# Layer B's keys and values by seven products for eight, for all heads, ahead of the attention

## The chip, the cores and the metric

The kernel runs on one core of one Trainium2 chip. The metric is the device time of one execution in microseconds (us). Before the change the median of three runs is 2861.07 us (2860.74 to 2862.50). The profile shown is of one execution of its own, which took 2862.76 us; the span from its first to its last instruction is 2861.1 us.

## The reference, cut to what matters

One step of a small encoder with two layers over 640 tokens (512 of a new stream, 16 each of 8 running streams), model width 2048. Layer A is a pooling mixer with an input projection 2048 -> 8192, four group maps and an output projection 4096 -> 2048. Then keys, values and one forget logit per head are made of the stream, and layer B attends to them:

```python
hk = rmsnorm(x, norm_kv)
kvf = hk @ w_kv                              # 2048 -> 16 heads x 128 keys, the same of values, 16 logits
k = kvf[..., :W_B].reshape(B, T, N_HEADS, HEAD_DIM)
v = kvf[..., W_B:2 * W_B].reshape(B, T, N_HEADS, HEAD_DIM)
logf = jax.nn.log_sigmoid(kvf[..., 2 * W_B:] + b_f)
...
F_all = jnp.cumsum(logf_all, axis=1)
for l in range(N_B):                         # one layer
    h = rmsnorm(x, norm_b[l])
    z = h @ w_in_b[l]                        # query and gate, 2048 each
    o = fox_attention(q, k_all, v_all, Fq, F_all, q_pos, k_pos)
    x = x + (o * jax.nn.silu(gate)) @ w_out_b[l]
return rmsnorm(x, norm_f), k, v, logf, ...
```

Keys, values and log forget values are outputs too. A running stream also attends to 256 cached rows per head. All matrices are float32.

## The kernel before

All activations lie with features on the 128 partitions and the 640 tokens along the row, as two halves of 320. Every large product is made of three TensorE products, from a value split into a rounded part "h" and a rest "l": h with h, h with l, l with h. `split` (L80) makes the two parts: ScalarE writes the rounded copy (L81), VectorE subtracts it (L84). One TensorE matmul here is a 128x128 block of a weight by 320 tokens.

**Layer A.** `pair8` (L244) makes 256 columns of an output by a scheme with seven block products in place of eight (Strassen-Winograd): the input's 2048 rows are four slabs, and in each slab the loop goes over seven products and two row blocks, three matmuls each: 42 matmuls a slab, 168 for a pair of column blocks. The seven results lie in PSUM banks 0 to 6 until `combine` (L263) adds them up on VectorE, after one ScalarE copy (L275). The weights of a slab arrive as one DMA of 512 KB into `raw` (three buffers, `fetch` L181), and `prep` (L196) makes their sums (VectorE L201, L203, L204) and splits all seven blocks (L81, L84). `advance` (L219) keeps this up to three or four slabs ahead, and `wbufs` (L188) hands out the buffers in turn, three in the input projection (loads 0 to 127, `NA`), four after it. The activations' seven blocks (`Side` L143) are split ahead: three in the tiles "bh", "bl", four sums in "th", "tl".

In the input projection `u_pair` (L493) and `gate_pair` (L595) alternate, 32 pairs in four groups of the pooling; a u pair ends in running sums on GpSimd (L545), one more of them in each later group. Group maps use `plain` (L626), without the seven products: 96 matmuls for 256 columns. The output projection uses the seven products for the first three groups (`out_pair` L662) and `plain` for the last (`last_pair` L763), eight pairs of 14 us each. `last_pair` adds its product to the stream that it has read back from memory, stores it, takes squares for the norm (ScalarE, then a sum on GpSimd, L740) and splits it into the operands of layer B (`split_x` L744; for the second half of the blocks after the loop).

**Layer B before the change.** `proj` (L864) makes 128 columns of a projection of the whole stream: 16 row blocks by three products by two halves, 96 matmuls (`mm3` L814, L817). `chunk` (L859) brings a quarter of the weights at a time (DMA of 256 KB, L832), scales it by the norm's gain (VectorE L838) and splits it (L846, L848), two chunks ahead. Each head has four such projections, of keys (`k_block` L939), values (`v_block` L949), gate (`gate_block` L1111) and query (`q_block` L1097). The norm's factor R of each token is multiplied onto the result. Keys and values are turned with VectorE's 32x32 transposes and stored as output rows (`key_rows`, `v_rows`); values come back from memory with tokens on partitions.

Attention of a head (`attn` L1142) is a Python generator. It is cut into 17 pieces by `yield`, and `tick` (L88) runs the next piece; `proj` calls `tick` after every second row block, that is every 12 matmuls, or calls `next` on the rows' generator. So a head's attention (scores of the cache L1150 and of new tokens L1158 to L1162, softmax, transposes L105, values L1249 to L1263) is woven into the key and value projections of the next head.

`forget` (L971) makes the forget logits once, at the start of layer B: 32 narrow matmuls by the float32 stream (L1018, `acc` is the whole stream, read back), logarithms and running sums.

**Order.** TensorE's program is in the order written (`manual_schedule`). For the other engines and the DMA queue of SyncE (SP) a planner puts instructions in order by its own costs; each engine then runs its list in order. Memory of a pool that was closed is handed on tile by tile when the last reader of each tile is done.

After layer B the output projection (L1321, 512 columns a matmul) and the last norm follow.

Of the kernel before, what the change touches and what calls it, by code (L numbers as in the profile page):

```python
# [39 lines left out]
def tile_yoco_step(ctx, tc, i, o):  # L40
# [89 lines left out]
    xt_ = pool(ctx, "xt")  # L130
    sa = ctx.enter_context(ExitStack())
    wa, xb_, misc = pool(sa, "wa"), pool(sa, "xb"), pool(sa, "misc")

    def tslot(j, part, shape, dt=F32):
        return xt_.tile(shape, dt, tag=f"t{part}{j}", name=f"t{part}")

    def bslot(j, part, shape, dt=F32):
        return xb_.tile(shape, dt, tag=f"b{part}{j}", name=f"b{part}")
# [16 lines left out]
    def blocks_b(sd, x4):  # L155
        sd.bh, sd.bl = (bslot(sd.j, q, [P, 3, HALF], F32R) for q in "hl")
        nc.scalar.activation(sd.bh, x4[:, 1:4, :], AF.Copy)
        nc.vector.tensor_tensor(sd.bl, x4[:, 1:4, :], sd.bh.bitcast(F32), op=ALU.subtract)
# [18 lines left out]
    NA = 128  # L177
# [9 lines left out]

    def wbufs(n, shape):  # L188

        j = n % 3 if n < NA else (2, 0, 3, 1)[(n - NA) % 4]  # L190
# [3 lines left out]
        return None, [[bslot(k, q, [shape[0], 1] + shape[2:], F32R) for k in range(2)] for q in "hl"]  # L194
# [24 lines left out]
    def advance():  # L219

        d = ndone[0]
        ahead = 3 if d < NA else 4
        while nprep[0] < min(d + ahead, len(loads)):
            if nload[0] <= nprep[0]:
                fetch()
            prep()
# [17 lines left out]
    def pair8(hook=None):  # L244

        pp = {m: banks[:, j, :] for j, m in enumerate(ORDER)}
        for s in range(4):
            wts = parts.pop(0)
            advance()
            for j, m in enumerate(ORDER):  # L250
                for kk in range(2):
                    product(pp[m], m, wts, kk, xs_[2 * s + kk], s + kk == 0, s == 3 and kk == 1)
                if j == 6:
                    done()
                if hook is not None:
                    hook(s, j)
# [43 lines left out]


# [5 lines left out]
    rows.append([bslot(4 + q // 2, "hl"[q % 2], [P, 512]) for q in range(4)])  # L307
    x4s = [tslot(4 + j // 2, "hl"[j % 2], [P, 4, HALF]) for j in range(7)] + [x4slot()]
    gains = [bslot(j, q, [1, 512]) for j in (2, 3) for q in "hl"]
    ones, idle = bslot(6, "h", [1, P]), bslot(6, "l", [P, P])  # L310
    ssq, tiny = bslot(7, "h", [P, TT, 4]), bslot(7, "l", [P, TT, 3])
# [314 lines left out]
    def plain(xk):  # L626
# [4 lines left out]
        for b in range(2):  # L631
            bk = [bank()[:, :HALF], bank()[:, :HALF]]
# [29 lines left out]
    def out_pair(g, c):  # L662
# [41 lines left out]
        o3 = bslot(2, "hl"[c % 2], [P, 3, HALF])  # L704
# [19 lines left out]
    ps_ = pool(sa, "ps_")  # L724
# [7 lines left out]
    xh, xl = [None] * KT, [None] * KT  # L732
    sqd = dram.tile([P, NT], F32, name="sqd")
    sqs = []

    def squares(k, x):
        s = bslot(2, "hl"[k % 2], [P, NT]) if k else misc.tile([P, NT], F32, tag="cve", name="sq")
        nc.scalar.activation(s, x, AF.Square)
        if k:
            nc.gpsimd.tensor_tensor(sqs[0], sqs[0], s, op=ALU.add)  # L740
        else:
            sqs.append(s)

    def split_x(k, x):  # L744

        t = tslot(k // 2, "hl"[k % 2], [P, 2, NT], F32R)
        xh[k], xl[k] = t[:, 0, :], t[:, 1, :]
        split(xh[k], xl[k], x)

    late = []  # L750

    def load_stream_pair(c):
        if c == 3:
            x1 = [bslot(3, q, [P, NT]) for q in "hl"]
        else:
            x1 = m4slot() if c in (2, 6) else x4slot() if c == 7 else ps_.tile([P, 4, HALF], F32, tag="sg", name="x1", bufs=2)
            x1 = x1.rearrange("p (k s) n -> p k (s n)", k=2)
            x1 = [x1[:, 0, :], x1[:, 1, :]]
        for k in range(2):
            dma(x1[k], xacc[c][k * P : (k + 1) * P, :])  # L760
        return x1

    def last_pair(c, x1, yk):  # L763
        pp = plain(yk)
        for b in range(2):
            a = halves(x1[b])
            for s in range(2):
                nc.vector.tensor_tensor(a[:, s, :], a[:, s, :], pp[b][s], op=ALU.add)
            k = 2 * c + b
            dma(xacc[c][b * P : (b + 1) * P, :], x1[b])  # L770
            squares(k, x1[b])
            if k < 8:
# [656 lines left out]
```

## Time and profile before

| stretch | us from the start | what runs |
|---|---|---|
| layer A, input projection | 0 to about 890 | 31 pairs by seven products, the first pair plain |
| layer A, group maps and output | 890 to 1524 | `plain`, `out_pair`, from about 1412 `last_pair` |
| layer B, keys, values, gate, query, attention | 1528 to 2633 | 64 projections and 16 heads |
| output projection and last norm | 2633 to 2861 | L1321 |

| | before |
|---|---|
| median of the runs | 2861.07 us |
| the profiled execution | 2862.76 us |
| its span | 2861.1 us |
| TensorE busy | 2800.3 us (98%) |
| VectorE, ScalarE, GpSimd busy | 65%, 35%, 11% |
| granted clock of TensorE, mean | 0.992 |

In the profile PE is TensorE, PEld its loading of weights, DVE VectorE, ACT ScalarE, POOL GpSimd and SP SyncE. A row of a group names the line, the engine, the operation, what is written and read, and how often. The end of a matmul is modelled, and matmuls overlap, so their pace is read from one start to the next and not from their durations. The row of a stretch gives for each engine its busy time and number of instructions, then TensorE's granted clock (1.00 is full), the busy share of the DMA engines and GB/s.

### The profile page before, as it was taken

Reading aid. Unit: us, or ns where it says so; the run is one execution under the profiler, and the core shown is the slowest. Engines: PE = TensorE matmul, PEld = TensorE weight load, DVE = VectorE, ACT = ScalarE, POOL = GpSimd, SP = SyncE. Lnnn points to the kernel's source line nnn. Section 1 sums busy time; section 2 is a strip of 40 time slices with the busy share of each in tenths; the row PEclk is TensorE's granted clock in tenths of the full one; section 3 lists DMA queues with packets and bytes.
Section 4 is the critical chain, followed back from the end, with each engine's and each line's share of the span. In section 5 each row is a group of like instructions: output and inputs, shape, how many; then the busy total and the mean of one; then the engine's idle time right before and its main releaser. Section 6 shows DMA issues by size and latency. Waiting matters only on the chain. (4 is left out here: it accounts for less than half of the span.)

```text
span 2861.1 us, 46583 instructions
## 1 busy us (share of the span) xinstructions
PE 2800.3 (98%) x18578; PEld 2698.3 (94%) x18578; DVE 1872.7 (65%) x3253; ACT 996.3 (35%) x1633; POOL 323.6 (11%) x333
## 2 busy tenths in 40 slices
PE   7899999999999999999999999999999999999998
PEld 6799999999999999999998999999999999999887
DVE  7877778888776848495445665566666665556434
ACT  5433333333333534343232233333333333334222
POOL 2212122232340110202021000000000000000000
PEclk9899999999999999999999999999999999999999
DMA  3344444444335786868636555444554545455833
GB/s 126 108 138 126 133 127 121 139 123 128 115 107 186 184 169 177 174 178 177 178 128 179 134 127 124 119 116 114 124 121 115 124 119 120 118 122 112 143 88 108
DMA packets 677058, 384.08 MB, mean 134 GB/s; under 512 B 323364, under 2 KB 634068, under 8 KB 676712
## 3 DMA queue, kind: packets, MB, share of 16 engines
q1 hardware_dynamic: 657256, 327.36, 43.2%
q0 software_dynamic: 19584, 53.75, 8.6%
q8 instruction: 145, 2.38, 0.3%
q14 instruction: 73, 0.60, 0.1%
HBM read 298.30 MB, written 82.71 MB: 133 GB/s over the span
## 5 line engine op out<-in xcount | busy, mean ns | idle before, releaser
L237 PE MATMUL banks<-th,wh 128*128 128x320 f32 x1280 | 404.9, 316 | 4.6 <-DVE cu L279 2.8
L817 PE MATMUL banks<-th,whi 128*128 128x320 f32 x2048 | 399.8, 317 | 3.5 <-ACT whi L846 3.5
L237 PE MATMUL banks<-th,wl 128*128 128x320 f32 x1280 | 400.2, 313 | 2.8 <-DVE wl L84 2.8
L237 PE MATMUL banks<-tl,wh 128*128 128x320 f32 x1280 | 399.8, 312 | 0.5 <-DVE tl L84 0.5
L817 PE MATMUL banks<-tl,whi 128*128 128x320 f32 x2048 | 385.0, 310 | 0.0
L848 DVE TENSOR_TENSOR wlo<-raw,whi 128x512 fp32r<-128x512 f32 x272 | 186.8, 687 | 216.0 <-ACT whi L846 212.8
L817 PEld LDWEIGHTS banks<-th,whi 128*128 128x128 f32 x2048 | 316.3, 189 | 9.7 <-ACT whi L846 3.8
L817 PEld LDWEIGHTS banks<-tl,whi 128*128 128x128 f32 x2048 | 322.9, 189 | 0.0
L237 PE MATMUL banks<-bh,wh 128*128 128x320 f32 x960 | 298.3, 311 | 14.6 <-ACT cve L275 10.7
L846 ACT ACTIVATE whi<-raw 128x512 fp32r<-128x512 f32 x272 | 171.6, 632 | 381.8 <-PE banks L817 226.7
L237 PE MATMUL banks<-bl,wh 128*128 128x320 f32 x960 | 297.6, 310 | 0.0
L237 PE MATMUL banks<-bh,wl 128*128 128x320 f32 x960 | 297.5, 310 | 0.0
L81 ACT ACTIVATE wh<-raw 128x768 fp32r<-128x768 f32 (+1 forms) x200 | 177.0, 887 | 336.8 <-issue 159.9
L84 DVE TENSOR_TENSOR wl<-raw,wh 128x768 fp32r<-128x768 f32 (+1 forms) x200 | 209.9, 1051 | 115.9 <-ACT wh L81 115.4
L81 ACT ACTIVATE wh<-sums 128x1024 fp32r<-128x1024 f32 x160 | 168.6, 1054 | 244.3 <-DVE sums L204 244.2
L237 PEld LDWEIGHTS banks<-th,wh 128*128 128x128 f32 x1280 | 244.4, 191 | 8.1 <-DVE cu L279 4.0
L237 PEld LDWEIGHTS banks<-th,wl 128*128 128x128 f32 x1280 | 244.2, 191 | 3.3 <-DVE wl L84 3.3
L237 PEld LDWEIGHTS banks<-tl,wh 128*128 128x128 f32 x1280 | 244.6, 191 | 0.8 <-DVE tl L84 0.8
L817 PE MATMUL banks<-th,wlo 128*128 128x320 f32 x1024 | 234.2, 310 | 2.0 <-DVE wlo L848 2.0
L84 DVE TENSOR_TENSOR wl<-sums,wh 128x1024 fp32r<-128x1024 f32 x160 | 202.9, 1268 | 48.0 <-ACT wh L81 47.6
L817 PE MATMUL banks<-tl,wlo 128*128 128x320 f32 x1024 | 234.1, 310 | 0.0
L237 PEld LDWEIGHTS banks<-bh,wh 128*128 128x128 f32 x960 | 181.3, 189 | 16.2 <-ACT cve L275 11.8
(407 smaller groups left out, 5285.9 us busy)
## 6 DMA issues: line engine op xcount, KB each, us to landing
raw<-in_w_in_a SPq DMA_DIRECT2D x128, 512.0 KB, 4.0
raw<-in_w_out_a SPq DMA_DIRECT2D x64, 512.0 KB, 4.7
raw<-in_w_kv SPq DMA_DIRECT2D x128, 256.0 KB, 3.2
raw<-in_w_in_b SPq DMA_DIRECT2D x128, 256.0 KB, 3.0
raw<-in_w_grp_a SPq DMA_DIRECT2D x32, 512.0 KB, 5.8
kc<-in_cache_k SPq DMA_DIRECT2D x64, 256.0 KB, 4.3
vc<-in_cache_v SPq DMA_DIRECT2D x16, 1024.0 KB, 7.6
raw<-in_w_out_b SPq DMA_DIRECT2D x64, 256.0 KB, 3.0
```

The source lines that it names most:

```text
L81: a = nc.scalar.activation(hi, x, AF.Copy)
L84: nc.vector.tensor_tensor(lo, x, hi.bitcast(F32), op=ALU.subtract)
L237: nc.tensor.matmul(bank[:, :HALF], w[kk][:, a, :], x, start=first and q == 0, stop=last and q == 2)
L817: nc.tensor.matmul(acc_[:, s, :HALF], w, x[:, s * HALF : (s + 1) * HALF], start=f, stop=l)
L846: nc.scalar.activation(hi, raw, AF.Copy)
L848: nc.vector.tensor_tensor(lo, raw, hi.bitcast(F32), op=ALU.subtract)
```

## The change

- **Keys and values first.** After layer A's last product a new stretch makes keys and values of all heads with `pair8` and `combine`: 16 calls of `kv_pair`, each two heads' keys or two heads' values. Their weights become 64 more loads of the list that layer A uses, of kind "s" (sums); `prep` scales them by the norm's gain with four ScalarE instructions ahead of the sums. `place` now says which weight buffer a load uses and which load has to be done before it.
- **The stream's operands** are the seven blocks of `Side` (`blocks_b`, `sums_t`, `split_t`), made during and after the eight `last_pair`s; `split_x` goes. Sums of sides 6 and 7 run on GpSimd. `last_pair` reads and stores the stream in one DMA each instead of two.
- **Result of a pair:** R is multiplied on by one GpSimd instruction on 128x1280; `rows_out`, one more generator, turns the result, stores keys to the outputs and to a scratch in memory (`kscr`), and values to a scratch (`sv`).
- **The forget logits'** narrow matmuls move into the `last_pair`s (`forget_sums`: four matmuls in each of the next one, on two instead of four column groups in turn); the rest of `forget` and the norm's factor run as pieces during the first pairs.
- **The attention part** has only the query and the gate as projections, 32 in place of 64. Each `proj` runs nine pieces (the last gate 16), after row blocks 0, 2, 4, 6, 8, 9, 11, 13 and 15. A head's attention starts in its own gate's projection and ends in the next head's query. The DMAs and splits that fetch the next head's keys, values, sums and cache stand at fixed places in `attn`.
- **Memory:** the operands are kept as "bh"/"bl" tiles (`xb_`) plus one more block per side (`last_blocks`, read back from memory during the last pair); `stream` picks the block. `R` and the running sums go through memory to the next part. The output projection's operands take over these places.

```diff
+    kvs = [(q, m) for m in range(8) for q in range(2)]
+    LAST = (3, 0, 1, 2)
+    for q, m in kvs:
+        for s in LAST if (q, m) == kvs[-1] else range(4):
+            c0 = q * D + m * 2 * P
+            loads.append(("s", wkv[:, 4 * s : 4 * s + 4, c0 : c0 + 2 * P], nkv_c[:, 4 * s : 4 * s + 4]))
...
     def prep():
         n = nprep[0]
-        raw = loaded.pop(n).rearrange("p (a b) (s n) -> p a (b s) n", a=2, n=P)
+        raw = loaded.pop(n)
+        if len(loads[n]) > 2:
+            for k in range(4):
+                nc.scalar.activation(raw[:, k, :], raw[:, k, :], AF.Copy, scale=loads[n][2][:, k : k + 1])
+        raw = raw.rearrange("p (a b) (s n) -> p a (b s) n", a=2, n=P)
...
+    def forget_sums(c):
+        for k in (2 * c, 2 * c + 1):
+            q = k % 4
+            for n in range(2):
+                nc.tensor.matmul(banks[32 * q : 32 * q + 32, 6 + n, :HALF], wr[0][:, k * H : k * H + 32],
+                                 stage[c][:, k % 2, n * HALF : (n + 1) * HALF], start=k < 4, stop=k >= 12)
...
-                last_pair(c, x1s[c], yk)
+                    load_stream_pair(q)
+                if c == 0:
+                    load_forget()
+                last_pair(c, yk)
+                if c:
+                    sums_t(x4of(c - 1)) if c < 7 else None
+                if 0 < c < 5:
+                    split_t(xs_[c - 1], x4of(c - 1))
         dk = nd
-    dma(sqd, sqs[0])
-    for k, x in late:
-        split_x(k, x)
+    for j in range(4, 7):
+        if j == 6:
+            blocks_b(xs_[j], x4of(j))
+            sums_t(x4of(j), None, nc.gpsimd)
+        split_t(xs_[j], x4of(j))
...
+    def kv_pair(n, q, m):
+        def hook(s, j):
+            if (n, s, j) == (0, 0, 2):
+                last_rows()
+            if (n, s, j) == (15, 2, 0):
+                last_blocks()
+
+        pp = pair8(hook, LAST if n == 15 else range(4))
...
+        t = x4slot()
+        combine(pp, lambda name: [(t[:, WHERE[name], :], slice(0, HALF))])
+        t = t.rearrange("p (k s) n -> p k (s n)", k=2)
+        nc.gpsimd.tensor_tensor(t, t, R.unsqueeze(1).to_broadcast([P, 2, NT]), op=ALU.mult)
+        work.insert(0, rows_out(q, m, t))
...
-    def proj(also=None):
+    def proj(ticks=9):
         pp = mmbank()
         for c in range(4):
             wh, wl = (w.rearrange("p (k n) -> p k n", n=P) for w in chunk())
             for k in range(4):
                 kk = 4 * c + k
-                mm3(pp, wh[:, k, :], wl[:, k, :], xh[kk], xl[kk], kk == 0, kk == KT - 1)
-                if kk % 2:
-                    if also is not None and kk > 1:
-                        next(also, None)
-                    if also is None or kk != 3:
-                        tick()
+                mm3(pp, wh[:, k, :], wl[:, k, :], kk, kk == 0, kk == KT - 1)
+                if kk * ticks % KT < ticks:
+                    tick()
         return pp
...
+        q_ = []
+        work.append(attn(0, q_))
         for h in range(H):
+            q_.extend(q_block(h))
             if h:
-                ks_ = k_block(h)
-                kc = load_keys(h)
-                vt = v_block(h, ks_[0])
-                sums = load_sums(h)
-                v, q_ = [], []
-                rows_ = v_rows(h, vt, v)
-                if h < H - 1:
-                    gate_block(h - 1, rows_)
-                vc = load_values(h)
-            work.append(attn(h, *ks_, v, q_, sums, kc, vc))
-            if h:
-                q_.extend(q_block(h))
-        gate_block(H - 2, rows_)
-        gate_block(H - 1)
+                work.append(attn(h, q_))
+            gate_block(h)
+            q_ = []
+        while work:
+            tick()
```

The step that follows `last_pair(7)` in the new order, run after the first 18 matmuls of the first key pair:

```diff
+    def last_rows():
+
+        forget_sums(7)
+        nc.scalar.activation(lt[:, :HALF], banks[:, 6, :HALF], AF.Copy)
+        nc.vector.tensor_copy(lt[:, HALF:], banks[:, 7, :HALF])
+        blocks_b(xs_[7], x4of(7))
+        sums_t(x4of(7), None, nc.gpsimd)
+        split_t(xs_[7], x4of(7))
```

More of the change, by code (lines that the diff above doesn't have):

```diff
@@ L631, in plain @@
         for b in range(2):
-            bk = [bank()[:, :HALF], bank()[:, :HALF]]
+            if c is None:
+                bk = [bank()[:, :HALF], bank()[:, :HALF]]
+            else:
+                bk = [banks[:, (4 * c + 2 * b + s) % 6, :HALF] for s in range(2)]
+            if b and c:
+                forget_sums(c - 1)
             for k in range(8):
```

564 lines of the change are left out of this document (301 added, 263 removed).

## The prediction

> **What bounds the kernel now.** I read the page's busy times first, then the chain of waits through layer B, then the stretches, and last the idle time before matmuls.
>
> ```profile
> PE 2800.3 (98%) x18578; PEld 2698.3 (94%) x18578; DVE 1872.7 (65%) x3253; ACT 996.3 (35%) x1633; POOL 323.6 (11%) x333
> ```
> ```profile
> 1832.12 29.91 PE banks L817 x204
> ```
> ```profile
> 1899.90 29.91 PE banks L817 x204
> ```
> ```profile
> 1000.00:1100.00 100.00, 100.00 (x684) 100.00 (x684) 60.81 (x98) 35.94 (x51) 15.17 (x15) 1.00 0.71 162
> 1764.35:1832.12 67.77, 67.77 (x476) 65.07 (x476) 40.45 (x80) 21.75 (x42) 0.00 (x0) 1.00 0.50 120
> 1794.26:1832.12 37.86, 37.86 (x272) 35.35 (x273) 25.25 (x55) 12.73 (x28) 0.00 (x0) 1.00 0.48 105
> ```
>
> TensorE ends every wait. A head takes 1899.90 - 1832.12 = 67.78 us, and TensorE is never idle in it. A projection's matmul costs 29.91/204 = 0.1466 us; in the stretch of layer A, where `out_pair` runs by seven products, 100/684 = 0.1462, so the two forms cost the same. A head's four projections are 384 x 0.1466 = 56.3 us, which leaves 11.5 us of attention matmuls. The last row is the part of a head in which its attention is woven in: as full as the rest, with VectorE busy for 25.25 of 37.86 us.
>
> **The change part by part.** The sum is made against the profiled span, 2861.1 us. That execution took 2862.76 us, 1.7 more than its span and 1.7 more than the median of the runs, so a span of 2861.1 stands for a median of 2861.07 and differences carry over.
>
> *Products.* Keys and values were 32 x 96 = 3072 matmuls; 16 pairs of 168 are 2688. 384 x 0.1466: **-56.3 us**. The weights' multiplication in gate and query stays.
>
> *The turn into layer B goes.*
>
> ```profile
> 1528.10 0.87 PE L817 MATMUL banks<-th,whi 128*128 128x320 f32 x4 [3.49 <-ACT whi L846]
> 1530.94 0.64 PE L817 MATMUL banks<-th,wlo 128*128 128x320 f32 x1 [1.96 <-DVE wlo L848]
> 1597.54 0.39 PE L1160 MATMUL banks<-kh,qh 128*128 128x256 f32 x1 [1.77 <-DVE pr L1164]
> ```
> ```profile
> 1530.00:1536.40 6.40, 5.46 (x20) 5.47 (x21) 4.46 (x9) 1.47 (x3) 5.14 (x17) 0.50 0.97 292
> 1560.00:1630.55 70.55, 68.78 (x510) 63.32 (x509) 43.82 (x104) 16.87 (x35) 0.00 (x0) 0.98 0.65 139
> ```
>
> TensorE idles 3.49 + 1.96 us and then runs 6.4 us at half clock, worth 3.2: 8.7. Head 0's first scores wait 1.77 more, and the clock of 0.98 over 70.55 us is another 1.4. I take **-11.9**.
>
> *Forget logits.*
>
> ```profile
> 1564.45 4.51 PE banks L1018 x64
> ```
> ```profile
> L1018 PE MATMUL banks<-acc,wr x64: 432/433/457, 1564.4 to 1568.5; 128*32 128x320 f32 x64
> ```
> ```profile
> 1861.97 1.06 PE L1150 MATMUL banks<-kct,qs 128*32 128x256 f32 x8
> 1862.96 0.49 PE L1158 MATMUL banks<-kt,qt 128*128 128x128 f32 x2
> ```
>
> The 64 instructions now come eight at a time, two column groups in turn instead of four. The cache scores L1150 have just that pattern: 8 in 0.99 us at 256 tokens, so 1.24 at 320, times 8 is 9.9 us. Bounds: the old pace, 4.5, and no overlap at all, 64 x 0.433 = 27.7. Net **+5.4** (0 to +23).
>
> *A steady key or value pair.* VectorE has per slab `prep`, per pair `combine` and two transposes; GpSimd has the product with R.
>
> ```profile
> L84 DVE TENSOR_TENSOR wl<-sums,wh 128x1024 fp32r<-128x1024 f32 x36 | 44.1, 1224 | 8.7 <-ACT wh L81 8.4
> L84 DVE TENSOR_TENSOR wl<-raw,wh 128x768 fp32r<-128x768 f32 x36 | 34.3, 954 | 22.7 <-ACT wh L81 22.7
> L201 DVE TENSOR_TENSOR sums<-raw 128x512 f32<-128x512 f32 x47 | 32.4, 689 | 9.4 <-DMA raw<-in_w_out_a 8.7
> L204 DVE TENSOR_TENSOR sums<-raw,sums 128x256 f32<-128x256 f32 x47 | 19.8, 422 | 0.7
> L203 DVE TENSOR_TENSOR sums<-sums,raw 128x256 f32<-128x256 f32 x47 | 19.8, 421 | 0.5
> ```
> ```profile
> L279 DVE TENSOR_TENSOR cu<-cu,banks 128x320 f32<-128x320 f32 x31 | 14.9, 482 | 0.0
> L934 DVE STREAM_TRANSPOSE kn<-kt 128x640 f32<-128x640 f32 x16 | 13.4, 836 | 0.0
> L740 POOL TENSOR_TENSOR sq<-sq,bl 128x640 f32<-128x640 f32 x8 | 14.0, 1754 | 90.4 <-ACT bl L738 90.4
> L545 POOL TENSOR_TENSOR sw<-sw 128x772 f32<-128x772 f32 (+2 forms) x48 | 85.6, 1783 | 4.8 <-DMA dscr<-dd 1.4
> L846 ACT ACTIVATE whi<-raw 128x512 fp32r<-128x512 f32 x272 | 171.6, 632 | 381.8 <-PE banks L817 226.7
> ```
>
> VectorE: 4 x 3.71 + 7 x 0.482 + 2 x 0.836 = 19.9 us beside 168 x 0.1466 = 24.6 us of TensorE. GpSimd: 128x1280, twice L740, 3.5 us. These two disturb each other:
>
> ```profile
> 685.80 6.17 POOL L545 TENSOR_TENSOR sw<-sw 128x772 f32<-128x772 f32 x3
> ```
> ```profile
> 686.84 1.84 DVE L201 TENSOR_TENSOR sums<-raw 128x512 f32<-128x512 f32 x1
> 688.72 1.57 DVE L203 TENSOR_TENSOR sums<-sums,raw 128x256 f32<-128x256 f32 x1
> 690.33 1.93 DVE L204 TENSOR_TENSOR sums<-raw,sums 128x256 f32<-128x256 f32 x1
> ```
>
> Beside GpSimd's sums the operations of 0.689, 0.421 and 0.422 us take 1.84, 1.57 and 1.93. So I count both engines' work in a row: 19.9 + 3.5 = 23.4 of 24.6 us, still under TensorE. The Trainium skill speaks against this part: "SBUF — State Buffer", section "Who interferes with whom", says that a VectorE instruction with two inputs in SBUF and a GpSimd one that reads SBUF block each other fully. By that rule too the sum in a row, 23.4, would hold, and the pair would stay TensorE's; the trace's tripled durations agree.
>
> ScalarE gets four 128x256 instructions a slab, each under the 0.632 of 128x512, at most 10 us a pair, spread over an engine that is busy for a third. The row stores move here too:
>
> ```profile
> L930 SPq DMA_DIRECT2D out_k_prompt<-kn x64: 327/490/1122, 1557.3 to 2563.5; - x64
> ```
>
> For a key pair SP issues 16 of these (8 for values), a store to the scratch and four weight loads, 21 x 0.49 = 10 us of its 24.6; a store queued ahead of a load waits for GpSimd and a transpose, some 6 us after the pair's end, and the weights are fetched up to three slabs, 18 us, ahead. I add 0.3 us a pair for waits on banks: **+4.5** (0 up to the first rival's price).
>
> *The new turn, `last_pair(7)` to the first key pair.* Nothing is spare here. Sides 4 to 7 are split late, since their places hold the last product's operands. From the end of that product until slab 3 of the first pair, 3 x 6.2 + 1.2 = 19.7 us later, VectorE and GpSimd have:
>
> ```profile
> L158 DVE TENSOR_TENSOR bl<-m,bh 128x960 fp32r<-128x960 f32 x12 | 13.9, 1156 | 0.0
> L84 DVE TENSOR_TENSOR tl<-draw,th 128x1280 fp32r<-128x1280 f32 x16 | 23.8, 1489 | 6.7 <-ACT th L81 6.7
> ```
>
> two `blocks_b` (2 x 1.156), two splits (2 x 1.489), two preps (2 x 3.71), two sums on GpSimd (8 halves of L740, 7.0), one square (1.75), two adds (1.0): 22.5 us, and the norm's factor beside it. Late by 3 to 6 us, then `forget`'s small operations in pairs 1 and 2 while VectorE has 1.2 us a pair to spare, and one or two stretches at half clock (1.5 each, below). I take **+10**, from 2 (hidden but for one bank wait) to 22 (all exposed). Queued behind each late VectorE subtraction are the next preps, and TensorE waits for them in order. What covers this work otherwise is TensorE's own 24.6 us of the first pair.
>
> *The turn into the attention part.* The new weight buffers lie where side 0's sums were, whose last reader is the second of four slabs of the last pair, 12 us before its end; so the first chunks can be split ahead. **+2.5** (0, to the old turn's 8.7).
>
> *Attention with half the projections.* 192 x 0.1466 + 11.5 = 39.6 us a head, already in the sum, if nothing waits. The quoted 37.86 us stretch is nearly this loop: two projections with the attention's pieces 12 matmuls apart, no idle time.
>
> ```profile
> L848 DVE TENSOR_TENSOR wlo<-raw,whi 128x512 fp32r<-128x512 f32 x272 | 186.8, 687 | 216.0 <-ACT whi L846 212.8
> L838 DVE TENSOR_TENSOR raw<-raw,cols 128x512 f32<-128x512 f32 x256 | 169.7, 678 | 5.3 <-DMA raw<-in_w_kv 3.9 <-DMA raw<-in_w_in_b 0.9
> ```
>
> VectorE drops by 8 x 1.365 and four operations of 0.84, from 40.4 to 26.1 us of 39.6, 66%, as in that stretch (67%). SP loses eight weight DMAs and 16 row stores a head; the value load's store behind its own load stays, and weights are two chunks, some 9 us, ahead of it. **+3** for 16 heads (0 to 32). The last head runs pieces 6 matmuls apart: **+2** (0 to 8).
>
> Sum: -56.3 - 11.9 + 5.4 + 4.5 + 10 + 2.5 + 3 + 2 = -40.8, so **2820 us**.
>
> **The rivals.**
>
> *Every pair stalls at its boundary (slower).* Layer A's fourth group does so:
>
> ```profile
> 415.16 0.42 ACT L275 ACTIVATE cve<-banks 128x320 f32<-128x320 f32 x1
> ```
> ```profile
> 465.00 0.42 ACT L275 ACTIVATE cve<-banks 128x320 f32<-128x320 f32 x1
> ```
> ```profile
> 697.86 0.42 ACT L275 ACTIVATE cve<-banks 128x320 f32<-128x320 f32 x1
> ```
> ```profile
> 752.98 0.42 ACT L275 ACTIVATE cve<-banks 128x320 f32<-128x320 f32 x1
> ```
> ```profile
> 698.34 0.41 PE L237 MATMUL banks<-bh,wh 128*128 128x320 f32 x1 [2.54 <-ACT cve L275]
> ```
> ```profile
> 699.70:703.10 3.40, 3.40 (x14) 3.40 (x15) 3.40 (x9) 0.53 (x1) 0.00 (x0) 0.56 0.35 120
> ```
>
> ScalarE's copy L275, behind a split that waits for VectorE, holds bank 0; TensorE idles 2.54 us and then loses 44% of 3.4 us, 1.5. Two units take 55.1 us (752.98 - 697.86) instead of 49.8 (465.00 - 415.16): 5.3 a stall. On all 16 pairs: 2820 - 4.5 + 85 = 2900. From 8 stalling pairs on, the gain is gone. For it: ScalarE has more ahead of its copy now. Against it: in a row, two units of that group have 36.4 us of VectorE and 14.3 of eight GpSimd sums, over TensorE's 49.3; two key pairs have 46.8. (On the clock, "TensorE: Matmul & The Clock Gate", section "HAM oscillation", of the Trainium skill asks for gaps above about 3.4 us; by it this stall would cost 2.5 only. The trace shows half clock after 2.54, and I price by the trace.)
>
> *Attention's own latency bounds a head.* With no plain projections between, a late softmax is never caught up. One wait like the 1.77 at head 0 in each head: +28 - 3, 2845. For it, that wait; against it, the 14 later heads without any.
>
> *The new turn is hidden.* Planner and buffers cover it: +2 for it, none at boundaries: 2807.
>
> **How the numbers follow.** Forecast with its own range 2808 to 2834: 0.68; hidden turn or better, 0.12; attention latency, 0.10; boundary stalls, 0.08, of which some stop short of slower; anything else 0.02. A measurement here can tell 0.2%, 6 us. Slower needs over 47 us against the sum: 0.06; the same 0.03; faster 0.91. The range 2800 to 2845 reaches over the hidden turn and attention latency and leaves boundary stalls out.
>
> **What would show it.** Right: 16 key and value pairs with starts 24.6 to 25.5 us apart after the first two; heads 39.6 to 40 us apart with TensorE full; about 10 us of idle and half clock in the first 50 us after the last L638 matmul; eight groups of forget matmuls of 1.2 us. Wrong: waits of TensorE for L275 in most pairs, a head above 41 us, or a granted clock below 0.98 in either part.

## The result, and the profile after

The changed kernel takes 2910.95 us (median of four runs, 2910.45 to 2913.13) against 2861.78 for the kernel before beside it: a ratio of 1.0171, 95% interval 1.0153 to 1.0189. It is slower by 1.7%; 2820 had been predicted. The profiled execution took 2911.26 us, its span 2909.3. Two executions of the experiments took far longer than the others of their kernel, 8918.69 us in run 9 and 3500.23 in run 12, and are left out of the medians given below.

The page's row of busy times, as it was shown of before:

```profile
PE 2780.2 (96%) x18194; PEld 2651.2 (91%) x18194; DVE 2014.5 (69%) x3430; ACT 1149.5 (40%) x1911; POOL 382.2 (13%) x357
```

The 384 matmuls are gone (18578 to 18194), but TensorE is busy for 96% instead of 98%: it waits. Four stretches, by engine (length; busy time and count of PE, PEld, DVE, ACT, POOL; clock; DMA):

```profile
1532.40:1630.00 97.60, 87.73 (x571) 84.65 (x571) 82.23 (x140) 51.74 (x87) 25.42 (x25) 0.95 0.40 99
1630.00:1955.00 325.00, 322.91 (x2163) 316.94 (x2163) 267.30 (x369) 172.41 (x304) 38.67 (x18) 1.00 0.52 122
1955.40:2073.80 118.40, 103.46 (x686) 95.07 (x685) 66.57 (x139) 36.06 (x72) 3.17 (x2) 0.96 0.61 146
2161.37:2248.98 87.61, 80.90 (x566) 73.78 (x565) 53.77 (x120) 33.04 (x66) 0.00 (x0) 1.00 0.54 130
```

The first is the turn from layer A into the first pairs of keys and values, the second is the rest of that part, nearly full. The third is the start of the attention part, the fourth two of its heads: 87.6 us at full clock, of which TensorE is idle for 6.7. VectorE is busy for 61% there, ScalarE for 38%, so no engine is at its limit.

To see where the 89 us between forecast (2820.3 of span) and result lie, I divide the span at TensorE's wait behind the last `last_pair` (1534.94 - 2.27 = 1532.67; before, 1528.10 - 3.49 = 1524.61) and at its wait for the attention part's first weights (1961.35 - 5.66 = 1955.69). TensorE's larger waits of the first turn and the first of the second (in brackets the idle time and what ended it):

```profile
1534.94 0.53 PE L251 MATMUL banks<-b,wh 128*128 128x320 f32 x2 [2.27 <-DVE x L802]
1544.66 1.41 PE L877 MATMUL banks<-sq,ones 128*128 128x320 f32 x2 [2.79 <-DVE lt L866]
1570.56 0.41 PE L251 MATMUL banks<-th,wh 128*128 128x320 f32 x1 [1.80 <-DVE cu L290]
1575.50 0.64 PE L251 MATMUL banks<-th,wh 128*128 128x320 f32 x1 [2.25 <-DVE cu L293]
1961.35 0.63 PE L1069 MATMUL banks<-th,whi 128*128 128x320 f32 x1 [5.66 <-ACT whi L1098]
```

The output projection of the kernel before starts at 2632.7 (its first row, below), 228.4 us ahead of the end, and I take as much off the end here. (That is a convention: a few of its matmuls now stand among the last head's work, from 2662.8 on.)

```profile
L1321 PEld LDWEIGHTS banks<-whi,th x240: 186/188/192, 2632.7 to 2794.9; 128*128 128x128 f32 x120
```

| stretch | forecast, us | measured, us |
|---|---|---|
| layer A to its end | 1534.5 (1524.6 + 9.9) | 1532.7 |
| keys and values | 408.6 (394.1 + 10 + 4.5) | 423.0 |
| attention part | 648.8 (the rest of the sum) | 725.2 (2909.3 - 228.4 - 1955.7) |

So 76 of the 89 us lie in the attention part. Its row holds the turn into it (+2.5 in the sum) and the last head (+2) too, but most of the 76 belongs to the term for all heads that I had put at +3. A steady head there (one row of VectorE's list, the gate's product, per head) takes 44.25 and 43.36 us and not 39.6:

```profile
2157.13 0.83 DVE L1371 TENSOR_TENSOR og<-og,sgb 128x640 f32<-128x640 f32 x1 [4.07 <-ACT og L1367]
2201.38 0.83 DVE L1371 TENSOR_TENSOR og<-og,sgb 128x640 f32<-128x640 f32 x1 [4.07 <-ACT og L1367]
2244.74 0.83 DVE L1371 TENSOR_TENSOR og<-og,sgb 128x640 f32<-128x640 f32 x1 [4.07 <-ACT og L1367]
```

TensorE's waits over the attention part up to 2640, grouped (total, times, longest):

```profile
PE banks L1069 <- ACT whi L1098: 36.0, 23, 5.7
PE banks L105 <- DVE pr L1259: 20.0, 14, 2.0
```

A projection's matmul (L1069) waits for ScalarE's rounded weights, and a transpose (L105) for a softmax row. With two single waits of 1.8 and 0.9 us these make 58.7 us; what else the 76 are made of was not taken apart, and half clock behind some waits is a part of it (0.96 granted in the third stretch). Now one wait for weights, followed back through the lists of PE, ScalarE, VectorE and SyncE:

```profile
2207.01 0.41 PE L1069 MATMUL banks<-tl,whi 128*128 128x320 f32 x1 [1.08 <-ACT whi L1098]
```
```profile
2206.33 0.63 ACT L1098 ACTIVATE whi<-raw 128x512 fp32r<-128x512 f32 x1 [2.60 <-DVE raw L1090]
```
```profile
2197.02 0.29 DVE L1353 COPY ob<-banks 128x128 f32<-128x128 f32 x1 [5.09 <-PE banks L1351]
...
2202.30 0.49 DVE L1187 SCALAR_TENSOR_TENSOR qt<-banks,R 128x320 f32<-128x320 f32 x1
...
2204.37 1.30 DVE L1232 STREAM_TRANSPOSE kct<-kc 128x512 f32<-128x512 f32 x2
2205.59 0.65 DVE L1090 TENSOR_TENSOR raw<-raw,cols 128x512 f32<-128x512 f32 x1
```
```profile
2182.41 1.28 SPq L1084 DMA_DIRECT2D raw<-in_w_in_b  x1
2188.55 2.50 SPq L1084 DMA_DIRECT2D raw<-in_w_in_b  x3
```
```profile
DMA to landing us min/median/max: 3.3/3.5/3.7
```

Four loads of chunks of weights are issued between 2182.41 and 2191 and land 3.3 to 3.7 us later (the last row is of these four). VectorE idles 5.09 us ahead of 2197.02 and, by the row of 2201.38 shown above, 4.07 us more, with the first chunk there since about 2186. But in its list the scale of the first chunk (L1090) stands behind the head's last products, the query's parts and two key transposes, at 2205.59, some 20 us after landing; ScalarE and TensorE wait behind it. The Trainium skill ("PSUM — Partial Sum Buffer", section "Engine vs sequencer instructions") calls the queues of ScalarE, VectorE and GpSimd strictly first in, first out; the trace agrees, as the ready scale does not pass the copy that waits 5.09 us.

### The profile page after: what moved, and what is told of

The parts are those of the page before. It is cut to its first block, busy times and chain, and to the rows that moved or that the text cites. A ratio compares the mean times of both kernels' runs of the same rounds, so it can differ in the third digit from the quotient of the medians.

```text
span 2909.3 us, 46312 instructions
## 1 busy us (share of the span) xinstructions
PE 2780.2 (96%) x18194; PEld 2651.2 (91%) x18194; DVE 2014.5 (69%) x3430; ACT 1149.5 (40%) x1911; POOL 382.2 (13%) x357
## 5 line engine op out<-in xcount | busy, mean ns | idle before, releaser
L251 PE MATMUL banks<-b,wh 128*128 128x320 f32 x2688 | 602.7, 311 | 16.7 <-ACT cve L289 10.6
L251 PE MATMUL banks<-th,wh 128*128 128x320 f32 x1792 | 566.9, 316 | 9.5 <-DVE cu L293 4.6
L251 PE MATMUL banks<-tl,wh 128*128 128x320 f32 x1792 | 557.6, 311 | 0.7 <-DVE tl L84 0.7
L251 PEld LDWEIGHTS banks<-b,wh 128*128 128x128 f32 x2688 | 452.5, 189 | 18.3 <-ACT cve L289 11.6
L251 PE MATMUL banks<-b,wl 128*128 128x320 f32 x1344 | 417.2, 310 | 0.0
L1069 PE MATMUL banks<-b,whi 128*128 128x320 f32 x1536 | 358.0, 317 | 0.0
L1069 PEld LDWEIGHTS banks<-b,whi 128*128 128x128 f32 x1536 | 257.8, 191 | 1.2 <-issue 0.4
L251 PEld LDWEIGHTS banks<-b,wl 128*128 128x128 f32 x1344 | 254.1, 189 | 0.0
L1069 PE MATMUL banks<-b,wlo 128*128 128x320 f32 x768 | 197.7, 312 | 0.0
L217 DVE TENSOR_TENSOR sums<-raw 128x512 f32<-128x512 f32 x236 | 174.9, 741 | 11.5 <-POOL sq L769 4.5
L1069 PEld LDWEIGHTS banks<-b,wlo 128*128 128x128 f32 x768 | 135.4, 190 | 0.0
```

What stands on the lines that cost most here:

```text
L217: nc.vector.tensor_tensor(sums[:, :, 0:2, :], raw[:, :, 1:3, :], raw[:, :, 0:1, :].to_broadcast([P, 2, 2, P]), op=ALU.subtract)
L251: nc.tensor.matmul(bank[:, :HALF], w[kk][:, a, :], x, start=first and q == 0, stop=last and q == 2)
L1069: nc.tensor.matmul(acc_[:, s, :HALF], w, stream(k, q, s), start=f, stop=l)
```

## The experiments

**Theories.** A: the order of VectorE's list is the loss; there is time enough. B: the softmax chains stand too densely, now that half the projections are gone, whatever the list. C: weights come late, because of the queue (C1) or too few buffers (C2).

**1. Program order for VectorE and ScalarE in the attention part.**

```diff
+        listed = ExitStack()
+        listed.enter_context(tc.manual_schedule(engines={mybir.EngineType.DVE, mybir.EngineType.Activation}))
         work.append(attn(0, q_))
```

> The changed kernel (2911 us) with one edit: in layer B's attention part VectorE and ScalarE run their instructions in the order in which the program issues them, and not in the planner's. Theory A (the weights' scale and split stand too late in VectorE's planned list, behind the query's parts and the key turns; VectorE has time enough): the three waits of a head for the rounded weights (1.08, 1.50 and 1.08 us) go, a head falls from 44.2 to 40 to 41 us, and the time to about 2850. Theory B (the softmax chains stand too densely for one wait after another, whatever the list): heads stay at 44 and the time at 2900 to 2920. If program order puts the softmax chains ahead of the weights' work instead, the time rises above 2920, and the list still decides.

3062.48 us, ratio 1.0701 (1.0683 to 1.0719). The last case of the expectation: the list decides, but this one is worse. Waits for rounded weights are gone but for the first (5.7 us), and TensorE waits for other things:

```profile
PE banks L105 <- DVE ptl L1270: 57.9, 23, 4.7
PE banks L1237 <- DVE kct L1232: 38.2, 12, 4.4
```

**2. Without the scale.**

```diff
-            nc.vector.tensor_tensor(r, r, braws[n][1].unsqueeze(2).to_broadcast([P, 4, P]), op=ALU.mult)
```

> The changed kernel with the multiplication of layer B's gate and query weights by the norm's gain left out (the output is another one): 8 multiplications of VectorE fewer per head. Theory A: the multiplication is the late link ahead of the rounding on ScalarE, so the waits for the rounded weights shrink or go and the time falls by 30 to 55 us, to 2856 to 2880. Theory B: VectorE is loaded to 61% in a head and the wait for a softmax row stays: the time falls by less than 15 us.

2909.51 us, 1.0169 (1.0148 to 1.0190): the time is the same, though VectorE has eight instructions of some 0.65 us less per head. The waits have moved:

```profile
PE banks L105 <- DVE pr L1258: 34.3, 14, 2.6
PE banks L1069 <- ACT whi L1097: 11.6, 16, 3.8
```

Those for rounded weights fell from 36.0 to 11.6 us, as A expected, and those for a softmax row rose from 20.0 to 34.3. The time is B's number. It removes the narrow form of A, that the scale by itself is the late link.

**3 and 4. More buffers.** Four instead of three for the rounded weights and rests, with three chunks prepared ahead instead of two; then seven instead of four for the incoming weights, with seven loads ahead (the main lines of each):

```diff
-        hi, lo = (wp.tile([P, 512], F32R, tag=q, name=q, bufs=3) for q in ("whi", "wlo"))
+        hi, lo = (wp.tile([P, 512], F32R, tag=q, name=q, bufs=4) for q in ("whi", "wlo"))
```
```diff
-            raw = wp.tile([P, 512], F32, tag="raw", name="raw", bufs=4)
+            raw = wp.tile([P, 512], F32, tag="raw", name="raw", bufs=7)
```

> The changed kernel with four buffers instead of three for the rounded and the rest weights, and three chunks prepared ahead of the first projection instead of two: a chunk is prepared one chunk of products (some 4.8 us) earlier. Theory A: a late scale then costs no wait; the time falls by 30 to 60 us, to 2850 to 2880. Theory B: no change beyond 10 us.

> The changed kernel with seven buffers instead of four for the weights as they come from memory, so that a chunk's load is issued three chunks (some 15 us) earlier. Theory C (the loads come late, behind other loads in SyncE's queue): the waits go and the time falls by 30 to 60 us. Theories A and B: the loads are there in time already, and the time moves by less than 10 us.

The first gives 2902.75 us, 1.0139 (1.0123 to 1.0154), 8 us less: again B's number. Its waits for rounded weights are nearly gone, but others stand in their place:

```profile
PE banks L105 <- DVE pr L1258: 20.0, 15, 1.6
PE banks L105 <- DVE ptl L1269: 15.5, 15, 1.0
PE banks L1069 <- ACT whi L1098: 7.2, 2, 5.7
```

These are softmax rows, rests of the turned softmax, and the weights. The second run gives 2868.09 us, 1.0017 (1.0008 to 1.0027), 43 us less than the changed kernel. That looked like C. But its list had changed as well: three scales in a row stand now at 2173.73, ahead of the head's end (L1371) by 15 us.

```profile
2173.73 1.88 DVE L1090 TENSOR_TENSOR raw<-raw,cols 128x512 f32<-128x512 f32 x3
...
2188.68 0.83 DVE L1371 TENSOR_TENSOR og<-og,sgb 128x640 f32<-128x640 f32 x1 [4.07 <-ACT og L1367]
```
```profile
PE banks L1237 <- DVE kct L1232: 19.6, 15, 4.5
```

What is left, but for the first wait of 5.7 us and two for a softmax row (2.8), are the waits for turned keys at a head's start.

**5, 6 and 8. Less to load; the scale issued earlier; the kernel before with more buffers.** Runs 5 and 6:

```diff
-                load_keys(h + 1)
+                cached[h + 1] = cached[h]
...
-            if more:
-                load_values(h + 1)
```
```diff
         split_next()
+        for n in range(3):
+            scale_next(n)
         fetchb()
```

> The changed kernel with four buffers for the incoming weights as it is, where the cached keys and values are loaded for the first head only (the 14 loads of the other heads, 1 MB each, are left out, so the output is another one). Theory C1 (the weights' loads stand behind the other loads of a head, in SyncE's queue and in what the planner reckons of it, so that their scale is listed late): without these loads the waits for the rounded weights go and the time falls by 30 to 45 us, as with seven buffers (2868). Theory C2 (four buffers are too few whatever else is loaded: a buffer is taken for a load, a scale, a rounding and a rest): the time falls by less than 10 us.

> The changed kernel with four buffers, where the program issues the scale of a chunk up to three chunks before it is rounded (in place, so no buffer more is needed). Theory A (the list: the scale is issued too late in the program and so listed too late): waits for the rounded weights go, 2868 to 2885. Theory C2 (a free buffer is missing for the next load): no change beyond 10 us, since the same four buffers are held as long.

> The kernel before with six buffers instead of four for layer B's incoming weights. If the change made the four buffers too few (the same chunks' preparation in half the time), the kernel before doesn't gain: 2855 to 2865. If four were too few in it already, it falls below 2840.

Run 5: 2908.95 us, 1.0156 (1.0141 to 1.0171). The time is the same without the cached keys and values of 15 heads (the expectation miscounts them as 14); the waits have gone over to the softmax rows:

```profile
PE banks L105 <- DVE pr L1259: 43.7, 15, 3.6
```

The waits for rounded weights went, as C1 expected (8.5 us are left of 36.0), but the time did not follow: the queue is not the loss, as the load followed above, landed 20 us ahead of its scale, says too. Run 6: 2916.24 us, 1.0181 (1.0166 to 1.0196): the planner put the scale back behind the key transposes (at 2209.86, behind two at 2208.64), so issuing it earlier in the program tests nothing but the planner.

Run 8, the edit of run 4 in the kernel before with `bufs=6`: 2882.72 us, 1.0063 (1.0048 to 1.0078): the kernel before gets slower with six buffers, which neither outcome of its expectation allowed. So more buffers are not a gain in themselves. As I read it, their number acts through the list that the planner makes with it, and C2 can't be read from run 4.

**7 and 10. The key transposes.** On seven buffers, the next head's first two transposes are issued near the end of a head, which then has two pieces fewer, each `proj` running eight (7), and then the query's parts are listed behind them (10):

```diff
             turn_new(3)
+            if more:
+                kc = cached[h + 1][0]
+                turned.append(pk.tile([P, NB * P], F32, tag="kct", name="kct"))
+                turn_keys(turned[0], 0, 0)
+                turn_keys(turned[0], 0, 1)
             yield
```
```diff
+            with tc.issue_after(tins[0]) if h else nullcontext():
                 nc.vector.scalar_tensor_tensor(qt[:, :HALF], pp[:, 0, :HALF], sc, R[:, :HALF], op0=ALU.mult, op1=ALU.mult)
```

> The kernel with seven buffers (2868 us) and one more edit: the first two transposes of a head's cached keys (1.30 us on VectorE) are issued near the end of the head before, where VectorE waits for 3.6 us, instead of at the head's start; a head has two steps fewer, and they are spread 12 products apart. If the waits of 1.3 us for the turned keys at each head's start (19.6 us in all) are what is left of the loss, they go and a head falls from 41.4 to about 40 us: 2845 to 2855, faster than the kernel before. If the wait moves to the next link (the query's parts or a softmax row), 2860 to 2870.

> The kernel with seven buffers and the early turn of the cached keys (2873.7 us), where the query's parts are now also listed behind these transposes, which the planner had put back behind them. Theory A: the 32.1 us of waits for turned keys go, a head falls from 42.1 to 39.7 to 40.5 us, and the time to 2838 to 2852. If another link of the head's start takes their place, 2860 or more.

Run 7: 2873.68 us, 1.0034 (1.0023 to 1.0046), no gain over run 4 and above both ranges of its expectation. VectorE waits 5.04 us for TensorE (ahead of 2190.02) in the head before, yet the transposes stand where they stood, behind the query's parts:

```profile
2196.85 0.28 DVE L1190 SCALAR_TENSOR_TENSOR qs<-banks,R 128x128 f32<-128x128 f32 x1
...
2198.25 1.30 DVE L1232 STREAM_TRANSPOSE kct<-kc 128x512 f32<-128x512 f32 x2
```

Run 10: 2886.37 us, 1.0086 (1.0071 to 1.0101), worse, against A's 2838 to 2852: TensorE now waits for the query's parts instead.

```profile
PE banks L1239 <- DVE qs L1191: 35.8, 15, 2.4
```

**9 and 13. The attention's steps and the query's parts listed behind the scales.** Four buffers, nothing else changed but this rule:

```diff
-            nc.vector.tensor_tensor(r, r, braws[n][1].unsqueeze(2).to_broadcast([P, 4, P]), op=ALU.mult)
+            a = nc.vector.tensor_tensor(r, r, braws[n][1].unsqueeze(2).to_broadcast([P, 4, P]), op=ALU.mult)
+            behind[:] = [a.ins]
...
+    def queued():
+        return tc.issue_after(behind[0]) if behind else nullcontext()
...
-                next(work[0])
+                with queued():
+                    next(work[0])
...
+            with queued():
                 nc.vector.scalar_tensor_tensor(qt[:, :HALF], pp[:, 0, :HALF], sc, R[:, :HALF], op0=ALU.mult, op1=ALU.mult)
```

> The changed kernel with four buffers; in layer B's attention part every VectorE instruction of the attention's steps and of the query's parts that the program issues after a weight scale is also listed behind that scale. Nothing else is ordered by hand. If the place of the scale in VectorE's list is the cause (theory A), the waits for the rounded weights go (36 us in the changed kernel) and the time falls to 2860 to 2880. If a scale listed earlier only makes VectorE wait for its load (theory C), waits on the loads appear in VectorE and the time stays above 2900.

> The same kernel as the run with the attention's steps and the query's parts listed behind the weights' scales (four buffers), for a profile in which a head can be read: 2845 to 2858. Theory A: no waits for rounded weights after the start, a head at 39.7 to 40.5 us, and the three scales of a head that stood behind the query's parts and the key turns now ahead of them.

2850.92 us (median of five), 0.9964 (0.9950 to 0.9978): 60 us less than the changed kernel, less than the 2860 that A expected at best, and less than the kernel before. Run 9 left no profile in which a head can be read; run 13 is the same kernel again, one execution of 2850.43 us. TensorE's two longest waits in its attention part:

```profile
PE banks L1245 <- DVE qs L1198: 12.4, 1, 12.4
PE banks L1075 <- ACT whi L1105: 5.7, 1, 5.7
```

With one of 1.8 us for turned keys that is all: the waits of the heads after the first are gone, for rounded weights and for softmax rows alike. A steady head, and what VectorE does around its end (the scale is L1096 here, the key transposes L1240):

```profile
2151.47 0.83 DVE L1379 TENSOR_TENSOR og<-og,sgb 128x640 f32<-128x640 f32 x1 [2.87 <-ACT og L1375]
...
2186.75 0.29 DVE L1361 COPY ob<-banks 128x128 f32<-128x128 f32 x1 [5.08 <-PE banks L1359]
...
2187.56 0.68 DVE L1096 TENSOR_TENSOR raw<-raw,cols 128x512 f32<-128x512 f32 x1
2191.11 0.83 DVE L1379 TENSOR_TENSOR og<-og,sgb 128x640 f32<-128x640 f32 x1 [2.87 <-ACT og L1375]
```
```profile
2151.47:2191.11 39.64, 39.64 (x285) 36.88 (x284) 26.98 (x59) 16.20 (x33) 0.00 (x0) 1.00 0.58 144
```

A head takes 39.64 us, TensorE full, with VectorE as busy as in the changed kernel (26.98 against 53.77/2 = 26.89 us). One scale stands in the gap ahead of the head's end, where the changed kernel had none. Of the three scales that the expectation names only this one comes ahead of the query's parts; in the head shown, the second comes behind them and ahead of the key transposes (2153.26), the third behind these (2156.29). B falls, and C2: the same chains, the same four buffers, the same loads. What the run shows is that the order is the loss. The planner made new lists for the whole part under the rule, so which of the places in it matters isn't shown; by run 2 the scale's place alone does not explain it.

**11, 14 and 15. The rule with the early key transposes of run 7, on four buffers; then from the second head on; then with the first weights loaded first.**

```diff
-            behind[:] = [a.ins]
+            if armed:
+                behind[:] = [a.ins]
```
```diff
-        dma(Fs, Fd)
...
         prime()
+        dma(R, Rd)
+        dma(Fs, Fd)
```

> Four buffers, the early turn of the cached keys, and the attention's steps and the query's parts listed behind the weights' scales. If buffers don't matter once the list is right, this equals the kernel with seven buffers and the keys first within 8 us. If they do, it stays 20 us or more above it.

> Four buffers, the early turn of the cached keys, and the attention's steps and the query's parts listed behind the weights' scales from the second head on only. In the run with this order from the first head on (2844.6 us), the query's parts of the first head came 11.1 us late, behind a scale whose load was under way. Theory A: that wait goes or shrinks to a few us, the other heads stay at 39.7: 2832 to 2840. If the first head's wait only moves to the rounded weights, 2842 to 2847.

> The kernel with the order from the second head on, where the first weights of the attention part are loaded ahead of the norm's factors R and the forget sums, which stood in front of them on SyncE's queue. Theory C for the start: the first wait for rounded weights (5.7 us) falls by 0.5 to 3 us, the rest is unchanged: 0 to 4 us below the kernel without this edit. If the loads wait for their memory and not for the queue, no change (within 1.5 us).

Run 11: 2844.63 us, 0.9940 (0.9925 to 0.9954), some 42 us below the kernel of run 10, not equal to it, and 29 below run 7, which has the same transposes and seven buffers without the rule: the rule is worth more than the buffers. Run 14: 2842.03 us, 0.9931 (0.9919 to 0.9942), the lowest, but not clearly apart from run 11 and above the 2832 to 2840 of theory A. Its first head still waits once for 7.2 us, now for a softmax row, instead of 11.1 for the query's parts:

```profile
PE banks L1256 <- DVE pr L1260: 7.2, 1, 7.2
PE banks L1075 <- ACT whi L1106: 5.7, 1, 5.7
PE banks L1246 <- DVE kct L1241: 1.8, 1, 1.8
```

These three are all of its waits in the attention part. Run 15: 2843.70 us, 0.9945 (0.9933 to 0.9958), no gain, and the first wait stays 5.7 us, though the first loads now start at 1953.36 instead of 1955.41 (run 14) and land 2.9 to 3.4 us after that. So neither the queue nor their memory is what this wait hangs on. The first scale starts at 1960.92 only, some 4 us after its load has landed: it stands behind a transpose of the last pair's values, which waits for GpSimd's product with R. The changed kernel has the same order:

```profile
1959.21 0.84 DVE L1008 STREAM_TRANSPOSE kn<-x 128x640 f32<-128x640 f32 x1 [3.00 <-POOL x L1032]
1959.98 1.25 DVE L1090 TENSOR_TENSOR raw<-raw,cols 128x512 f32<-128x512 f32 x2
```

That is a matter of VectorE's list once more; no run tried another order there.

**12. No weights to prepare.**

```diff
+        if used[0] <= 8 * H:
+            return bparts[0]
```

> The changed kernel where the gate and query products of all heads use the weights of the first chunk (the loads, scales, roundings and rests of the other 127 are left out; the output is another one). What is left of a head is the products and the attention's own work. If the weights' preparation is the whole loss, a head takes 39.7 to 40.5 us and the time is 2830 to 2845. If the attention's chains lose time by themselves at this density (theory B), a head stays above 42 us and the time above 2870.

2836.53 us (median of three), 0.9913 (0.9897 to 0.9930), a head 39.62 us:

```profile
2136.88 0.83 DVE L1378 TENSOR_TENSOR og<-og,sgb 128x640 f32<-128x640 f32 x1 [4.07 <-ACT og L1374]
2176.50 0.83 DVE L1378 TENSOR_TENSOR og<-og,sgb 128x640 f32<-128x640 f32 x1 [4.07 <-ACT og L1374]
```

So with the planner's own list the attention's chains alone lose nothing. Preparation loses 0.02 us a head under the rule of run 13 and about 4 under the planner's list (2244.74 - 2157.13 = 87.61 for two). Divided as in the table above, the attention part takes 651.3 us here (2834.6 - 228.4 - 1954.9), beside 725.2 in the changed kernel and 648.8 in the forecast.

**16. The kernel before under the same rule,** there for `next(also, None)`, the query's parts and the product of keys and R too.

```diff
+                        with queued():
                             next(also, None)
```

> The kernel before, with the same rule of order in its attention part: steps, query's parts and key scaling listed behind the weights' scales. Its heads show no waits for rounded weights, so if the late scale is a loss that the change brought, the kernel before gains nothing: 2855 to 2866. If the order by itself is worth something without the change, it falls below 2852.

2867.36 us, 1.0019 (1.0010 to 1.0027), just above the expected 2866: without the change the rule gains nothing. The change with the rule, 2851, is 11 us faster than the kernel before; with the early transposes as well, 2842, it is 20.

## Why the prediction was wrong, point by point

- **The failed step is "Attention with half the projections: +3 (0 to 32)".** It measured about +75: the 3 and the 76 of the table, less some 4.5 of the turn into this part (below). The step had the path of the weights wrong: it took VectorE's spare time for a guarantee that their preparation keeps ahead of TensorE. My argument was that a head's active stretch of before, "37.86 of 37.86", with VectorE busy for 67%, is nearly this loop. Its shares were right: 39.6 us a head from 192 matmuls and 11.5 us of attention is what runs 12 and 13 show (39.62, 39.64), and the whole part without preparation takes 651.3 us (run 12), 2.5 more than its sum. But a share of busy time says nothing of order. In the kernel before the planner's list happened to hold the weights' work early enough (from 1560 on TensorE has two waits there, of 1.8 and 1.3 us, both for VectorE's softmax work); the new loop got a new list, in which the scale came some 20 us after its data. That "weights are two chunks, some 9 us, ahead" held for the program, not for the list. The bound of 32 us was two microseconds a head; nothing in the profile of before could have bounded what a planner does with another loop, and the range should have said so. The sign named for it was right: a head above 41 us.
- **The rival "attention's own latency", 2845,** had the right place with the wrong cause. It named a softmax wait, of which 20.0 us are there, but in the heads after the first these too go when the list is right (run 13).
- **Products, -56.3:** right; 18578 - 18194 = 384.
- **Forget logits:** predicted 1.24 us for eight. Measured are 1.20 from the first's start to that of the matmul behind them (1447.97); the busy time of the row is 1.28, with a modelled end:

```profile
1446.77 1.28 PE L786 MATMUL banks<-x,wr 128*32 128x320 f32 x8
```

- **A steady pair, +0.3 us:** ScalarE's copy at a pair's end, first and last of a run of twelve:

```profile
1648.27 0.42 ACT L289 ACTIVATE cve<-banks 128x320 f32<-128x320 f32 x1
...
1928.85 0.42 ACT L289 ACTIVATE cve<-banks 128x320 f32<-128x320 f32 x1
```

 280.58/11 = 25.5 us a pair, 0.9 over the products, at the edge of the 24.6 to 25.5 that I gave, and three times the +0.3 of the sum. What the 0.9 is made of stays open: TensorE runs only the pairs' own products there, and its waits are a small part. The rival of a stall at each pair (5.3 us) is false: TensorE never waits for the copy, and from 1630 on it waits for VectorE's part of `combine` for 1.3 us in all.
- **The new turn, +10 (2 to 22):** the key and value part is 423.0 - 394.1 = 28.9 us above its products. With 0.9 x 16 = 14 of it at the pairs, about 15 are left for the turn: the waits of 2.27, 2.79, 1.80 and 2.25 us and half clock behind some of them. Inside its bounds, mis-sized by 5; the steady pairs are mis-sized by more, 14 against 4.5.
- **The turn into the attention part, +2.5 (0 to 8.7):** 5.66 us of wait for the first weights; it is the same under every order tried. The clock of 0.59 over the 3.4 us behind it adds 1.4, so that the term is inside its bounds and mis-sized by some 4.5. That "the first chunks can be split ahead" did not hold: their scale stands in VectorE's list behind the last pair's transpose (run 15).
- **Signs:** with the rule and the early key transposes (run 14) the forecast's sum is off by 22 us (2842 against 2820), most of it in keys and values, and the direction is right. That kernel has two changes more than the one forecast, so it does not make the forecast right. What I called the change was the change with a list that it did not bring along.

## What to carry to other kernels

When a loop is shortened around work that a planner orders, check the new list before believing shares of busy time: for each operand of the bounding engine compare when its data landed with when its first instruction stands in the list. A wait whose data has landed long before, beside an idle engine, is an order and not a load; deeper buffers may cure it by accident (2868) or make it worse (2882.7 for the kernel before), while one rule of order that puts the operand's preparation ahead of the other steps cured it with the buffers there were. Pinning everything cost more than the planner's fault (3062 against 2911), and pinning the wrong pair made a kernel slower too (2886 against 2874).

## What the runs showed of the hardware that was not expected

TensorE's clock falls after short waits here too. This stretch follows the wait of 2.79 us at 1544.66:

```profile
1544.66:1548.06 3.40, 3.40 (x12) 3.01 (x13) 3.35 (x5) 1.68 (x2) 3.26 (x7) 0.55 0.53 141
```

The granted clock is 0.55 over 3.4 us; in the 3.46 us ahead of the wait it was 1.00. The Trainium skill ("TensorE: Matmul & The Clock Gate", section "HAM oscillation") has the clock fall after gaps above about 3.4 us; the trace disagrees, and goes by a shorter one. Behind the wait of 1.80 us at 1570.56 it is lower as well:

```profile
1570.56:1573.20 2.64, 2.64 (x12) 2.29 (x12) 1.66 (x5) 2.64 (x6) 0.00 (x0) 0.70 0.60 162
```

There the starts of matmuls move from 0.15 us apart to 0.27 at about 1571.7, so the half clock began before the wait of 2.25 us at 1575.50, through which it was 0.50. Not every wait of that size does it: none was seen behind the wait of 2.27 us at 1534.94, whose 3.4 us ran at 1.00.

```profile
1534.94:1538.34 3.40, 3.40 (x24) 2.91 (x26) 1.13 (x2) 0.00 (x0) 3.17 (x4) 1.00 0.51 194
```

What stays open: why the planner lists the scale so late. Its costs are not in the trace, and no run here changed them.
